# Later seven-product cases in the first phases, none in the last phase, and an earlier scaling of the first tokens

## The chip, the cores and the metric

One NeuronCore of one Trainium2 chip runs the kernel. The metric is the device time of one execution in microseconds (us), as a median of several runs. A hardware profile of one execution stands beside it.

## The reference, cut to what matters

A trunk of two decoder layers over 256 tokens of width 2048, in float32. Only the last step of the second layer, its gated feed-forward, and the final norm are touched:

```
def conv_ffn(h, w_up, cw, cb, w_down):
    a = h @ w_up                                   # 2048 -> 2 x 5632
    c = causal depthwise conv of width 3 over a, + cb
    gate, val = c[..., :D_FF], c[..., D_FF:]
    return (jax.nn.silu(gate) * val) @ w_down      # 5632 -> 2048

x = x + conv_ffn(rmsnorm(x, g_ffn[l]), ...)
return rmsnorm(x, g_final)
```

## The kernel before

Every float32 product is made of three matmuls on split operands: a number is kept as a high part and the rest, and the product is high x high + high x rest + rest x high. A weight chunk of 128 rows and 1024 columns is loaded by SyncE's queue into a `raw` tile (four of them), ScalarE (ACT in the profile) writes its high part `whi` (four tiles), and VectorE (DVE) subtracts to get `wlo` (five tiles).

The feed-forward of the second layer (`ffn(1)`) runs in three parts over the 5632 inner columns (`FF_GROUPS = (4, 4, 3)`, times 512 columns). A part is an up-projection, whose groups end in evictions, convolution, SiLU and a product with the `gate` tile (two of them), and then a down-projection `down_phase`, called twice: phase one makes output columns 0 to 1023, phase two the rest. The down-projection has tokens on the output's partitions. Its inner dimension is taken in cases of 256 rows (eight cases in parts one and two, six in part three), and a case multiplies a 2x2 block matrix of activations (two blocks of 128 tokens, two blocks of 128 rows) with a 2x2 block matrix of weights (two blocks of rows, two halves of 512 columns).

- A plain case makes the eight block products, 24 matmuls of 128x512, into four PSUM banks `e00`, `e01`, `e10`, `e11` (token block, column half). On the weights it costs two ACT and two DVE operations of 128x1024 (`parts`, L707 and L708).
- A fast case (`fast_pair`) makes seven products, 21 matmuls, into seven banks (`e00`, `e01`, `e10` and `m1`, `m5`, `m6`, `m7`). Before its weights are split, DVE makes four sums of 128x512 (`xs`, L721); then three chunks of 1024 and one of 512 columns (`we`) are split. Its two weight chunks go to `raw` tiles in the first fast case of phase one, and otherwise to the two `gate` tiles, which are free only after the last product with the gate (`hv`, L872) of the up-projection.
- After a phase's last fast case `between` copies the four m banks to `staged` by ACT (L1358); `combine` adds them to the tokens `xt` by six DVE operations (L1366). Parts one and two postpone `combine` into the next up-projection. In part three phase one runs it with the first eviction, and phase two runs it at once in `between`.
- `evict` (L1385) adds an e bank to `xt`. In part three it also has ACT square the 512 columns (L1401, column block j of four), multiplies them by the final gain (L1405), and at block j = 2 makes most of the variance (L1407, L1408). `finish` scales one token block by its root (two blocks by ACT in L1424, two by DVE in L1425 and L1426) and stores it.

The order of the cases, and which are fast, stands in the table `FF_FAST`: for eight cases and for six, for each phase, the fast cases and the order. Within a down-projection the DMA, ACT and DVE steps on weights are chained in that order (`behind`); everything else, and TensorE's matmuls, is placed by the scheduler that builds the program. Only the last two cases of part three's phase two (`late=2`) are written out by hand: first all their products for `e00`, then `e01`, `e10`, and `e11` in two pieces of 256 columns, each followed by its eviction.

Of the kernel before, what the change touches and what calls it, by code (L numbers as in the profile page):

```python
# [13 lines left out]
ALU = mybir.AluOpType  # L14
# [17 lines left out]
EPS = 1e-6  # L32
FF_GROUPS = (4, 4, 3)
FF_FAST = {
    4: (((2, 3, 4), (0, 1, 2, 5, 3, 6, 7, 4)), ((2, 3, 4), (0, 1, 2, 5, 3, 6, 7, 4))),
    3: (((1, 2), (0, 1, 3, 2, 4, 5)), ((1,), (0, 1, 2, 3, 4, 5))),
}


# [34 lines left out]
class Kernel:  # L74
# [664 lines left out]


    def down_phase(self, dn, col, order, fast, lhs, rhs, pool, fp, between, evict, finish, late=0, late_gains=None):
        mm = self.nc.tensor.matmul
        names = ("m1", "m5", "m6", "m7"), ("e00", "e01", "e10", "e11")
        acc = {n: self.psum() for group in names[::-1] for n in group}
        left, right = slice(0, 512), slice(512, 1024)
        todo = {n: 0 for n in acc}
        for k in order:
            for n in ("m1", "m5", "m6", "m7", "e00", "e01", "e10") if k in fast else names[1]:
                todo[n] += 1 if k in fast else 2
        total = dict(todo)  # L750

        def three(n, x, w, out=None, ends=None):
            (xh, xl), (wh, wl) = x, w
            start, stop = (todo[n] == total[n], todo[n] == 1) if ends is None else ends
            todo[n] -= 1
            o = acc[n] if out is None else out
            mm(o, xh, wh, start=start, stop=False)  # L757
            mm(o, xh, wl, start=False, stop=False)  # L758
            mm(o, xl, wh, start=False, stop=stop)  # L759

        def plain(k, ws, tb, half, **kw):
            cols = (left, right)[half]
            for i, (wh, wl) in enumerate(ws):
                three(f"e{tb}{half}", lhs(2 * k + i, tb), (wh[:, cols], wl[:, cols]), **kw)

        kept = []
        last_fast = [k for k in order if k in fast][-1]
        for n, k in enumerate(order):
            raws = []
            for i in range(2):  # L770
                if k in fast and (col or k != fast[0]):
                    raw = self.tmp(fp, [P, 1024], "gate", 2)
                else:
                    raw = self.wp.tile([P, 1024], F32, tag="raw", name=self.uid("raw"), bufs=4)
                self.behind(self.nc.sync.dma_start(out=raw, in_=dn[(2 * k + i) * P : (2 * k + i + 1) * P, col : col + 1024]))
                raws.append(raw)
            if late_gains is not None and 2 <= n:
                late_gains(n - 2)
            if k in fast:
                names7 = "e00", "e01", "e10", "m6", "m5", "m7", "m1"  # L780
                for name, q, w in zip(names7, (1, 6, 2, 5, 4, 3, 0), self.fast_pair(raws, pool)):
                    three(name, rhs(k, q), w)
                if k == last_fast:
                    between([acc[m] for m in names[0]])
            else:
                ws = self.plain_pair(raws)
                if n < len(order) - late:
                    for tb in range(2):
                        for half in range(2):
                            plain(k, ws, tb, half)  # L790
                else:
                    kept.append((k, ws))
        if not late:
            for tb in range(2):
                for half in range(2):
                    evict(tb, half, acc[f"e{tb}{half}"])
            return
        ET = mybir.EngineType
        with self.tc.manual_schedule(engines={ET.PE, ET.DVE, ET.Activation}):
            for half in range(2):  # L800
                for k, ws in kept:
                    plain(k, ws, 0, half)
                evict(0, half, acc[f"e0{half}"])
            for k, ws in kept:
                plain(k, ws, 1, 0)
            evict(1, 0, acc["e10"])
            finish(0)
            for k, ws in kept[:-1]:
                plain(k, ws, 1, 1)
            k, ws = kept[-1]  # L810
            e, rest = acc["e11"], self.psum()
            for i, (wh, wl) in enumerate(ws):
                three("e11", lhs(2 * k + i, 1), (wh[:, 512:768], wl[:, 512:768]), out=e[:, :256], ends=(False, i == 1))
            evict(1, 1, e, 0)
            for i, (wh, wl) in enumerate(ws):
                three("e11", lhs(2 * k + i, 1), (wh[:, 768:], wl[:, 768:]), out=rest[:, 256:], ends=(i == 0, i == 1))
            evict(1, 1, rest, 1)
            finish(1)
# [491 lines left out]
class Tokens:  # L1310
# [45 lines left out]
    def between(self, accs):  # L1356
        for i, acc in enumerate(accs):
            self.nc.scalar.activation(self.staged[:, self.ph, i, :], acc, AF.Copy)  # L1358
        if self.last and self.ph:
            self.combine(1)  # L1360
        else:
            self.waiting.append(self.ph)

    def combine(self, ph):
        xt, m = self.xt, self.staged[:, ph]
# [10 lines left out]
        waiting, self.waiting = self.waiting, []  # L1376
        return {2 + 3 * i: [lambda ph=ph: self.combine(ph)] for i, ph in enumerate(waiting)}

    def evict(self, tb, half, acc, piece=None):
        k, nc, xt, sums = self.k, self.nc, self.xt, self.sums  # L1380
        j = 2 * self.ph + half
        c0, n = (0, 512) if piece is None else (256 * piece, 256)
        c = slice(j * 512 + c0, j * 512 + c0 + n)
        o = xt[:, tb, c]
# [9 lines left out]
        part, r, q, v, gb = self.part, self.r, self.q, self.v, self.gb  # L1394
# [6 lines left out]
            nc.scalar.activation(junk[:, :n], o, AF.Square, accum_out=sums[:, tb, j : j + 1])  # L1401
        if piece == 0:
            add(xt[:, tb, j * 512 + 256 : (j + 1) * 512], acc[:, 256:])
        if j < 3:
            nc.vector.tensor_tensor(o, o, gb[:, c], ALU.mult)  # L1405
        if j == 2:
            nc.vector.tensor_reduce(one(part), sums[:, tb, 0:3], AX.X, ALU.add)  # L1407
            nc.vector.tensor_scalar(one(part), one(part), -0.5 / D, -0.5 * EPS, ALU.mult, ALU.add)  # L1408
            nc.scalar.activation(one(r), one(part), AF.Sqrt, scale=-2.0)
        if j == 3:  # L1410
            if piece != 1:
                total = one(part) if piece == 0 else one(v)
                nc.vector.tensor_scalar(total, sums[:, tb, 3:4], -0.5 / D, one(part), ALU.mult, ALU.add)
            if piece == 0:
                return
            nc.scalar.activation(one(r), one(v), AF.Sqrt, scale=-2.0)
            nc.vector.reciprocal(one(r), one(r))
            nc.vector.scalar_tensor_tensor(one(q), one(r), one(r), one(v), ALU.mult, ALU.mult)
            nc.vector.scalar_tensor_tensor(one(r), one(q), 1.5, one(r), ALU.add, ALU.mult)
# [36 lines left out]
```

## Time and profile before

| | |
|---|---|
| median of 3 runs | 2053.24 us (2052.44 to 2053.37) |
| the profiled execution, its own time | 2053.55 us |
| its span from first to last instruction | 2051.8 us |
| mean granted TensorE clock | 0.997 |
| busy: TensorE matmul, VectorE, ScalarE, GpSimd | 99%, 73%, 54%, 7% |
| first down-projection matmul of part one, of part three | 1496.66 us, 1969.56 us |
| last matmul of the kernel, start | 2042.20 us |

Times are microseconds from the span's start. A row of the timeline gives start, duration, engine (PE is TensorE, SPq SyncE's queue), line and operation, and in brackets how long the engine had been idle and what ended that. Matmuls are pipelined, so a matmul's own duration is longer than the distance from one start to the next. A row of the chain gives start, length and what the chain ran through.

### The profile page before, as it was taken

The numbers are of one execution on the slowest core, as the hardware profiler recorded it, in microseconds if no ns is written. First come the engines' busy times: TensorE is split into PE (matmuls) and PEld (weight loads), VectorE is DVE, ScalarE is ACT, GpSimd is POOL, SyncE is SP. The second block draws the span as 40 slices with busy tenths as digits, with TensorE's granted clock in tenths as the row PEclk, the third lists the DMA queues.
The fourth block names the chain that finished last, engine by engine and source line by source line (L and its number), as shares of the span: only waits on it lengthen the run. The fifth ranks groups of instructions, "written<-read, shape, count | busy, mean of one in ns | idle before, by whom it ended". The sixth has DMA issues, their size and how long they took to land.

```text
span 2051.8 us, 39921 instructions
## 1 busy us (share of the span) xinstructions
PE 2034.3 (99%) x16229; PEld 1965.7 (96%) x16229; DVE 1504.8 (73%) x2280; ACT 1113.9 (54%) x1611; POOL 142.5 (7%) x200
## 2 busy tenths in 40 slices
PE   9999999999999999999999999999999999999997
PEld 8989999999999999999999999999988999889986
DVE  5866767767656766557788787777788777888778
ACT  6754744555435555345555675455555555555555
POOL 0000013000000000000043241300000000000000
PEclk9999999999999999999999999999999999999999
DMA  8876556666666666666665634678756666657653
GB/s 246 237 214 184 165 193 190 195 195 195 195 194 189 197 194 195 195 195 192 195 191 183 181 119 156 187 204 215 215 195 192 200 195 195 204 184 204 193 189 134
DMA packets 234253, 394.68 MB, mean 192 GB/s; under 512 B 53902, under 2 KB 61396, under 8 KB 234068
## 3 DMA queue, kind: packets, MB, share of 16 engines
q1 hardware_dynamic: 233876, 391.58, 63.6%
q8 instruction: 127, 2.08, 0.4%
q14 instruction: 58, 0.48, 0.1%
q10 hardware_dynamic: 192, 0.54, 0.1%
HBM read 387.88 MB, written 2.10 MB: 190 GB/s over the span
## 4 chain that ended last, share of the span: by engine, by line
PE 94%; DVE 3%; ACT 1%; DMA 1%; issue 0%; ACTq 0%
PE ps L156 26%; PE ps L157 26%; PE ps L159 26%; PE ps L758 2%; PE ps L759 2%; PE ps L757 2%; PE ps L188 2%; PE ps L189 2%; PE ps L190 2%; DVE wlo L708 1%; PE ps L523 1%; DVE xs L721 1%; DMA gate<-in_w_ffn_down 1%; ACT whi L707 0%; PE ps L603 0%
## 5 line engine op out<-in xcount | busy, mean ns | idle before, releaser
L118 DVE TENSOR_TENSOR wlo<-raw,whi 128x1024 fp32r<-128x1024 f32 x572 | 710.4, 1245 | 385.3 <-ACT whi L117 380.8
L117 ACT ACTIVATE whi<-raw 128x1024 fp32r<-128x1024 f32 x572 | 607.0, 1062 | 687.2 <-PE ps L157 586.6
L156 PE MATMUL ps<-xhl,whi 128*128 128x256 f32 x3264 | 762.8, 277 | 0.0
L157 PE MATMUL ps<-xhl,whi 128*128 128x256 f32 x3264 | 761.4, 276 | 0.0
L156 PEld LDWEIGHTS ps<-xhl,whi 128*128 128x128 f32 x3264 | 612.9, 188 | 0.4
L157 PEld LDWEIGHTS ps<-xhl,whi 128*128 128x128 f32 x3264 | 612.7, 188 | 0.4
L159 PE MATMUL ps<-xhl,wlo 128*128 128x256 f32 x3264 | 436.5, 276 | 0.0
L159 PEld LDWEIGHTS ps<-xhl,wlo 128*128 128x128 f32 x3264 | 400.5, 188 | 0.0
L156 PE MATMUL ps<-h,whi 128*128 128x256 f32 x704 | 163.6, 276 | 0.0
L157 PE MATMUL ps<-h,whi 128*128 128x256 f32 x704 | 163.6, 276 | 0.0
L157 PEld LDWEIGHTS ps<-h,whi 128*128 128x128 f32 x704 | 131.9, 188 | 0.0
L156 PEld LDWEIGHTS ps<-h,whi 128*128 128x128 f32 x704 | 131.9, 188 | 0.0
L156 PE MATMUL ps<-mainhl,whi 128*128 128x256 f32 x512 | 119.6, 277 | 0.0
L157 PE MATMUL ps<-mainhl,whi 128*128 128x256 f32 x512 | 119.4, 277 | 0.0
L853 ACT ACTIVATE c<-a,cT 128x256 f32<-128x256 f32 x176 | 99.2, 589 | 6.6 <-DVE a L236 6.5
L157 PEld LDWEIGHTS ps<-mainhl,whi 128*128 128x128 f32 x512 | 96.0, 188 | 0.0
L156 PEld LDWEIGHTS ps<-mainhl,whi 128*128 128x128 f32 x512 | 95.9, 188 | 0.0
L159 PE MATMUL ps<-h,wlo 128*128 128x256 f32 x704 | 94.1, 276 | 0.0
L758 PE MATMUL ps<-wlo,h 128*128 128x512 f32 (+1 forms) x228 | 89.5, 393 | 1.3 <-DVE wlo L708 1.3
L708 DVE TENSOR_TENSOR wlo<-raw,whi 128x1024 fp32r<-128x1024 f32 x61 | 73.5, 1222 | 21.8 <-ACT whi L707 21.3
L759 PE MATMUL ps<-whi,h 128*128 128x512 f32 (+1 forms) x228 | 89.1, 391 | 0.0
L707 ACT ACTIVATE whi<-raw 128x1024 fp32r<-128x1024 f32 x61 | 64.1, 1057 | 43.8 <-PE ps L759 20.8
(372 smaller groups left out, 2732.0 us busy)
## 6 DMA issues: line engine op xcount, KB each, us to landing
raw<-in_w_ffn_up SPq DMA_DIRECT2D x352, 512.0 KB, 4.2
raw<-in_w_ffn_down SPq DMA_DIRECT2D x152, 512.0 KB, 4.6
raw<-in_w_out SPq DMA_DIRECT2D x64, 512.0 KB, 4.5
raw<-in_w_in_a SPq DMA_DIRECT2D x56, 512.0 KB, 4.5
raw<-in_w_mem_kv SPq DMA_DIRECT2D x31, 512.0 KB, 4.8
gate<-in_w_ffn_down SPq DMA_DIRECT2D x24, 512.0 KB, 7.0
raw<-in_w_in_b SPq DMA_DIRECT2D x16, 512.0 KB, 4.6
raw<-in_w_kv_a SPq DMA_DIRECT2D x9, 512.0 KB, 5.0
```

The source lines that it names most:

```text
L117: nc.scalar.activation(hi[:, :n], raw[:, :n], AF.Copy)
L118: nc.vector.tensor_tensor(lo[:, :n], raw[:, :n], hi[:, :n].bitcast(F32), ALU.subtract)
L156: mm(acc[:, :S], wh, x[:, :S], start=first, stop=False)
L157: mm(acc[:, :S], wh, x[:, S:], start=False, stop=False)
L159: mm(acc[:, :S], wl, x[:, :S], start=False, stop=last)
L188: mm(acc, xh, wh, start=first, stop=False)
L189: mm(acc, xh, wl, start=False, stop=False)
L707: self.behind(self.nc.scalar.activation(hi, w, AF.Copy))
L708: self.behind(self.nc.vector.tensor_tensor(lo, w, hi.bitcast(F32), ALU.subtract))
L758: mm(o, xh, wl, start=False, stop=False)
L759: mm(o, xl, wh, start=False, stop=stop)
L853: nc.scalar.activation(c, a, AF.Identity, scale=w(2), bias=w(3))
```

## The change

Three things change. The order in phase one: with eight cases the fast ones move from places 2, 4 and 7 (counted from 0) to places 3, 5 and 7; with six cases from places 1 and 3 to places 2 and 5. Part three's phase two, which had case 1 fast, has no fast case, so that it allocates only the four e banks, `between` isn't called there, and `combine` isn't run for it. And in the tail `finish(0)` moves into the eviction of `e10`, behind ACT's square and ahead of the gain and the variance; the gain of that block moves behind the variance.

```diff
 FF_FAST = {
-    4: (((2, 3, 4), (0, 1, 2, 5, 3, 6, 7, 4)), ((2, 3, 4), (0, 1, 2, 5, 3, 6, 7, 4))),
-    3: (((1, 2), (0, 1, 3, 2, 4, 5)), ((1,), (0, 1, 2, 3, 4, 5))),
+    4: (((2, 3, 4), (0, 1, 5, 2, 6, 3, 7, 4)), ((2, 3, 4), (0, 1, 2, 5, 3, 6, 7, 4))),
+    3: (((1, 2), (0, 3, 1, 4, 5, 2)), ((), (0, 1, 2, 3, 4, 5))),
 }
...
-        acc = {n: self.psum() for group in names[::-1] for n in group}
+        acc = {n: self.psum() for group in (names[::-1] if fast else names[1:]) for n in group}
...
-        last_fast = [k for k in order if k in fast][-1]
+        last_fast = [k for k in order if k in fast][-1:]
...
-                if k == last_fast:
+                if k in last_fast:
                     between([acc[m] for m in names[0]])
...
-            evict(1, 0, acc["e10"])
-            finish(0)
+            evict(1, 0, acc["e10"], meanwhile=lambda: finish(0))
...
     def between(self, accs):
         for i, acc in enumerate(accs):
             self.nc.scalar.activation(self.staged[:, self.ph, i, :], acc, AF.Copy)
-        if self.last and self.ph:
-            self.combine(1)
-        else:
-            self.waiting.append(self.ph)
+        self.waiting.append(self.ph)
...
-    def evict(self, tb, half, acc, piece=None):
+    def evict(self, tb, half, acc, piece=None, meanwhile=lambda: None):
...
-        if j < 3:
+        meanwhile()
+        if j < 3 and not (tb and j == 2):
             nc.vector.tensor_tensor(o, o, gb[:, c], ALU.mult)
         if j == 2:
             nc.vector.tensor_reduce(one(part), sums[:, tb, 0:3], AX.X, ALU.add)
             nc.vector.tensor_scalar(one(part), one(part), -0.5 / D, -0.5 * EPS, ALU.mult, ALU.add)
             nc.scalar.activation(one(r), one(part), AF.Sqrt, scale=-2.0)
+            if tb:
+                nc.vector.tensor_tensor(o, o, gb[:, c], ALU.mult)
```

On VectorE, in phase one of part one, the last read of the up-projection's gate tile (`hv_2548`) stood behind the whole splitting of fast case 2, whose last row is the first one here, and behind a split of case 5.

```order
L708 TENSOR_TENSOR wlo_2580_18854<-xs_2572_18836,whi_2579_18853 128x1024
L855 SCALAR_TENSOR_TENSOR c_2547_18743<-a_2546_18741,cT_75,c_2547_18743 128x254
L872 TENSOR_TENSOR hv_2545_18737<-gate_2472_18194,c_2544_18733 128x256
L708 TENSOR_TENSOR wlo_2584_18883<-raw_2581_18878,whi_2583_18882 128x1024
L872 TENSOR_TENSOR hv_2548_18747<-gate_2472_18194,c_2547_18743 128x256
L708 TENSOR_TENSOR wlo_2586_18887<-raw_2582_18880,whi_2585_18886 128x1024
```

Now the same place reads as follows; the two L708 rows are the splits of plain case 5.

```order
L708 TENSOR_TENSOR wlo_2573_18837<-raw_2570_18832,whi_2572_18836 128x1024
L854 SCALAR_TENSOR_TENSOR c_2547_18743<-a_2546_18741,cT_75,c_2547_18743 128x254
L708 TENSOR_TENSOR wlo_2575_18841<-raw_2571_18834,whi_2574_18840 128x1024
L721 TENSOR_TENSOR xs_2578_18872<-raw_2576_18868 128x512
L721 TENSOR_TENSOR xs_2578_18872<-raw_2576_18868,raw_2577_18870 128x512
L245 TENSOR_TENSOR hx_2235_16487<-hv_2545_18737,hx_2235_16487 128x256
L871 TENSOR_TENSOR hv_2548_18747<-gate_2472_18194,c_2547_18743 128x256
L721 TENSOR_TENSOR xs_2579_18873<-xs_2578_18872,raw_2577_18870 128x512
L245 TENSOR_TENSOR hx_2235_16487<-hv_2548_18747,hx_2235_16487 128x256
L721 TENSOR_TENSOR xs_2579_18873<-xs_2579_18873,raw_2577_18870 128x512
```

The last gate read has moved ahead of fast case 2's four splits, and behind the splits of case 5 and two of case 2's four sums.

On SyncE's queue, in phase one of part three, the loads of the final gain (`gb`) stand between those of the weights; the two `gate` loads are the second fast case's.

```order
L775 DMA gate_24146<-in_w_ffn_down 128x1024
L775 DMA gate_24148<-in_w_ffn_down 128x1024
L1354 DMA gb<-in_g_final 128x512
L775 DMA raw_24197<-in_w_ffn_down 128x1024
L775 DMA raw_24199<-in_w_ffn_down 128x1024
L1354 DMA gb<-in_g_final 128x512
L775 DMA raw_24234<-in_w_ffn_down 128x1024
L775 DMA raw_24236<-in_w_ffn_down 128x1024
```

Now the two plain cases' loads stand first.

```order
L775 DMA raw_24146<-in_w_ffn_down 128x1024
L775 DMA raw_24148<-in_w_ffn_down 128x1024
L1353 DMA gb<-in_g_final 128x512
L775 DMA raw_24183<-in_w_ffn_down 128x1024
L775 DMA raw_24185<-in_w_ffn_down 128x1024
L1353 DMA gb<-in_g_final 128x512
L775 DMA gate_24220<-in_w_ffn_down 128x1024
L775 DMA gate_24222<-in_w_ffn_down 128x1024
```

The gate loads have moved behind four raw loads, those of plain cases 4 and 5.

On VectorE in the tail, from the eviction of `e10` to those of `e11` (`ps` names are the banks):

```order
L1385 TENSOR_TENSOR xt<-ps_24295,xt 128x512
L1405 TENSOR_TENSOR xt<-xt,gb 128x512
L1407 TENSOR_REDUCE fpart<-fsums 128x1
L1408 TENSOR_SCALAR fpart<-fpart 128x1
L1425 TENSOR_SCALAR xt<-xt,froot 128x512
L1426 SCALAR_TENSOR_TENSOR xt<-xt,froot,gb 128x512
L1385 TENSOR_TENSOR xt<-ps_24296,xt 128x256 x2
```

After the change (lines shifted by the edit):

```order
L1381 TENSOR_TENSOR xt<-ps_24295,xt 128x512
L1424 TENSOR_SCALAR xt<-xt,froot 128x512
L1425 SCALAR_TENSOR_TENSOR xt<-xt,froot,gb 128x512
L1404 TENSOR_REDUCE fpart<-fsums 128x1
L1405 TENSOR_SCALAR fpart<-fpart 128x1
L1408 TENSOR_TENSOR xt<-xt,gb 128x512
L1381 TENSOR_TENSOR xt<-ps_24296,xt 128x256 x2
```

The two scalings of `finish(0)` have moved directly behind the eviction, ahead of the variance and the gain.

## The prediction

> **What bounds the kernel now.** I read the page first, then TensorE's waits, then its timeline at each wait, and last the chain at those places. The page says that TensorE is nearly always at work and that the chain that ended last runs through it.
>
> ```profile
> PE 2034.3 (99%) x16229; PEld 1965.7 (96%) x16229; DVE 1504.8 (73%) x2280; ACT 1113.9 (54%) x1611; POOL 142.5 (7%) x200
> PE 94%; DVE 3%; ACT 1%; DMA 1%; issue 0%; ACTq 0%
> ```
>
> So a change can gain only where TensorE idles or is slow, or behind its last matmul. These are all the waits of TensorE from 1400 us to the end, by who ended them:
>
> ```profile
> PE ps L757 <- ACT whi L707: 5.0, 4, 2.5
> PE ps L758 <- DVE wlo L708: 1.3, 1, 1.3
> PE ps L757 <- ACT staged L1358: 0.2, 1, 0.2
> ```
>
> The timeline has them at six places, all in the second layer's down-projections (the brackets), between the first and the last matmul of part three, and two rows of an undisturbed stretch:
>
> ```profile
> 1519.36 0.74 PE L757 MATMUL ps<-whi,h 128*128 128x512 f32 x2 [0.75 <-ACT whi L707]
> ...
> 1777.54 0.74 PE L757 MATMUL ps<-whi,h 128*128 128x512 f32 x2 [0.70 <-ACT whi L707]
> ...
> 1969.56 0.40 PE L757 MATMUL ps<-whi,h 128*128 128x512 f32 x1
> ...
> 1987.85 0.73 PE L757 MATMUL ps<-whi,h 128*128 128x512 f32 x2 [2.47 <-ACT whi L707]
> ...
> 1989.93 0.79 PE L757 MATMUL ps<-whi,h 128*128 128x512 f32 x1 [1.05 <-ACT whi L707]
> ...
> 2017.52 0.51 PE L757 MATMUL ps<-whi,h 128*128 128x512 f32 x1 [0.23 <-ACT staged L1358]
> ...
> 2033.46 0.51 PE L758 MATMUL ps<-wlo,h 128*128 128x512 f32 x1 [1.28 <-DVE wlo L708]
> ...
> 2036.13 0.39 PE L757 MATMUL ps<-whi,h 128*128 128x512 f32 x1
> ...
> 2040.66 0.39 PE L759 MATMUL ps<-whi,h 128*128 128x512 f32 x1
> 2040.89 0.28 PE L757 MATMUL ps<-whi,h 128*128 128x256 f32 x1
> ...
> 2042.20 0.28 PE L759 MATMUL ps<-whi,h 128*128 128x256 f32 x1
> ```
>
> The rows at 2036.13 and 2040.66 are 20 undisturbed matmuls apart: 4.53 / 20 = 0.2265 us for each. Part three has 138 + 141 matmuls, six of them split into twelve of 256 columns. 273 x 0.2265 + 1.31 us for the twelve (11 steps to the last start, 2040.89 to 2042.20) is 63.15 us, but from 1969.56 to 2042.20 it took 72.64. **Part three loses 9.5 us**, of which the brackets name 5.0. Much of the rest is the clock, the last column but two here (it is 1.00 in the stretches around):
>
> ```profile
> 1989.00:1996.00 7.00, 6.07 (x15) 4.78 (x16) 6.08 (x6) 4.31 (x5) 0.00 (x0) 0.51 0.87 329
> ```
>
> What lies behind the waits is in the chain, and in SyncE's row for the two gate loads:
>
> ```profile
> 1511.69 4.40 DMA gate<-in_w_ffn_down
> 1516.12 1.31 DVE xs L721 x2
> ...
> 1519.36 0.74 PE ps L757 x2
> ```
> ```profile
> 1966.61 16.46 SPq L775 DMA_DIRECT2D gate<-in_w_ffn_down x2
> ```
> ```profile
> 1982.30 0.42 DVE L872 TENSOR_TENSOR hv<-gate,c 128x256 f32<-128x256 f32 x1
> ...
> 1986.68 0.69 DVE L721 TENSOR_TENSOR xs<-gate,gate 128x512 f32<-128x512 f32 x1 [3.06 <-DMA gate<-in_w_ffn_down]
> ```
>
> The second fast case can't load before VectorE's last product with the gate tile; that product stands behind the first fast case's splits; the load takes 3.9 to 4.4 us; then sums and splits follow. This is what ends last at the first four places.
>
> **The change part by part.** Durations of VectorE's rows, from all of the second layer's down-projections (starts follow some 0.08 us sooner than durations say):
>
> ```profile
> L708 DVE TENSOR_TENSOR wlo<-raw,whi 128x1024 fp32r<-128x1024 f32 x61 | 73.5, 1222 | 21.8 <-ACT whi L707 21.3
> ...
> L854 DVE SCALAR_TENSOR_TENSOR c<-a,cT,c 128x255 f32<-128x255 f32 x60 | 27.3, 478 | 0.0
> ...
> L1366 DVE TENSOR_TENSOR xt<-xt,staged 128x1024 f32<-128x1024 f32 x12 | 14.6, 1216 | 0.0
> ...
> L721 DVE TENSOR_TENSOR xs<-gate 128x512 f32<-128x512 f32 x12 | 8.2, 684 | 0.0
> ```
>
> *Parts one and two, first phases.* The last work of the up-projection, the last gate read of part one, and all engines' share of the time around them:
>
> ```profile
> 1496.18 0.76 DVE L236 TENSOR_TENSOR a<-ps,rbc 128x256 f32<-128x256 f32 x2 [0.63 <-PE ps L159]
> ...
> 1511.24 0.42 DVE L872 TENSOR_TENSOR hv<-gate,c 128x256 f32<-128x256 f32 x1
> ```
> ```profile
> 1494.00:1526.00 32.00, 31.25 (x150) 25.99 (x150) 28.59 (x44) 17.88 (x24) 0.00 (x0) 1.00 0.57 196
> ```
>
> Ahead of the last gate read VectorE now has, from 1496.18, three splits (1.14 each, 3.4 us), eight convolution steps (0.40, 3.2), eleven short operations (0.34, 3.7) and two sums (1.2): 11.5 us, to about 1508 instead of 1511.7. The load lands near 1512.5. TensorE starts case 3 after four plain cases and one fast, 117 matmuls or 26.5 us from the part's first at 1496.66: 1523.2, not 1517.7. The splits of case 3 are then held only by free `whi` tiles, and are over by 1523.5, while the last of them is needed at 1527. Both waits go, each with its slow restart (0.74 us for two matmuls instead of 0.45): **1.0 us each, 2.0 in all**. What is late next is case 4, whose gate tiles now come free only one plain case ahead: free at about 1521, landed 1525.5, summed 1530, split by 1534, needed from 1533.4 (first operand) to 1537. If nothing goes, 0; that is the other bound.
>
> *Part three, phase one.* VectorE's 15.3 us of work from 1969.2 to the last gate read put it at 1984.5, two later than before; the load lands at 1988.5. But the second fast case now starts after 117 matmuls, 1996.1, instead of 69. Its third operand gets a `whi` tile only when case 4 and most of 5 are through, at 1995.4; plus 1.06 (ACT) and 1.22 (DVE) it is ready at 1997.7, and needed 17 matmuls into the case, 1999.9. So both waits and the half clock go.
>
> *Part three, the seam.* The m banks are now done only at the phase's end. By the order the new `e00` takes the old `e00`'s bank, and `e01`, `e10`, `e11` those of m1, m6 and m5, which ACT's copies free:
>
> ```profile
> L1358 ACT ACTIVATE staged<-ps x24: 575/598/607, 1537.5 to 2023.5; 128x512 f32<-128x512 f32 x24
> ```
>
> m1 is copied by 1999.8, m6 by 2000.3, m5 by 2001.8; TensorE wants their banks at 2001.8, 2002.7 and 2005.6. I take 0. The bounds are 0 and all four copies, 2.4 us. `combine` (4.7 us of VectorE) runs beside the first plain cases, whose splits it delays by less than their lead.
>
> *Part three, phase two.* 24 matmuls stand for 21: 3 x 0.2265 = **0.7 us more**. VectorE loses four sums, a split and a half, and `combine`, which delayed the split at 2033.46; the copies at 2017.52 go too. What comes next is the pair of last cases for `e00`: by the order the `whi` tiles for case 5 come free four matmuls and one matmul before they start. Two ACT splits and a DVE split later the last `wlo` is there 2.8 us into the stretch, and is wanted after ten matmuls, 2.3: **0.5 us stays**. The bounds are 0 and the 1.5 of today (1.28 and the restart). So of 9.5 us, 9.0 go.
>
> *The tail.*
>
> ```profile
> 2039.73 0.69 DVE L1385 TENSOR_TENSOR xt<-ps,xt 128x512 f32<-128x512 f32 x1
> ...
> 2041.21 0.69 DVE L1405 TENSOR_TENSOR xt<-xt,gb 128x512 f32<-128x512 f32 x1 [0.79 <-ACT fjunk L1401]
> ...
> 2042.08 0.48 DVE L1425 TENSOR_SCALAR xt<-xt,froot 128x512 f32<-128x512 f32 x1
> 2042.47 0.75 DVE L1426 SCALAR_TENSOR_TENSOR xt<-xt,froot,gb 128x512 f32<-128x512 f32 x1
> 2043.13 0.75 DVE L1385 TENSOR_TENSOR xt<-ps,xt 128x256 f32<-128x256 f32 x2
> ```
>
> VectorE waited 0.79 us for ACT's square, then did gain, variance and both scalings before `e11`'s first piece, which TensorE had finished at 2041.8. The two scalings, 1.05 us, now fill that wait; the variance starts 0.2 late (2041.4), and `e11` starts at about 2042.4. ACT does its two scalings right behind the square too, so its square of `e11` comes as much sooner: **0.75 us** less. The bounds are 0, if the last piece's matmul ends the chain, and 1.0.
>
> *Sum.* 2.0 + 9.0 - 0.7 + 0.75 = 11.05. The profiled execution took 2053.55 (span 2051.8 and 1.75 around it), 0.31 above the median: 2042.5 in its terms, **2042.2 as a median**.
>
> **A rule beside the rows.** The clock fell after idles of 2.47 and 1.05 us, with 0.51 granted for 7 us, so what a wait of that size costs is by the rows itself plus about 3.4 us. The Trainium skill, "TensorE: Matmul & The Clock Gate", section on HAM oscillation, says that gaps in TensorE's work longer than about 3.4 us are what bring the half clock back. This trace differs: no single gap here was that long. By the page a wait of 2.5 us left in part three would cost only itself.
>
> **The rivals.** *The second fast case stays late in part three.* VectorE may fall behind its work as counted (it was busy 28.6 of 32 us around 1510), or a load may take longer. A wait of 2.5 us and its half clock, 5.9 us, then stay: 2048.1. Against it speaks that VectorE's long idle at that place was for the load, 3.06 us, and that the lead is now 2.2 us and more. 10%. By the page's rule it would be 2044.7, inside the forecast's range.
>
> *The gate tiles' round trip becomes the bound.* In parts one and two only case 7 (24 matmuls, 5.4 us) lies between fast cases 3 and 4. From the split that frees the gate tile the way is load 4.4, sums 2.4, ACT 1.06, DVE 1.22: 9.1 us. If that split comes only when TensorE starts case 7, and not 6 us ahead as I count, TensorE waits 3.6 us, and with the half clock 7.0, in each part: 2042.2 + 14.1 = 2056.3, slower. From a split about 2.5 us ahead of case 7 downward there is a wait. 4%.
>
> *The change does not do what it says.* The waits move by a place and come back nearly whole at the next fast case and at the seam (2.4 us of copies, and half clock): about 2050.5. 4%.
>
> **How the numbers follow.** The forecast holds 82%. With all waits gone and the tail at its best it is 2041.4; with three quarters of each upper bound taken up (2.0, 2.4, 1.0 and 0.75 us, in all 6.15) it is 2046.8. The runs before lie within 0.9 us of each other, so half of that is put outside the best case: the range is 2040.8 to 2047.0 and leaves out the rivals' 18%. A measurement of this kernel tells 0.2% (4.1 us) from no change: faster means below 2049.1. Faster 0.90 (the forecast and most of the first rival), same 0.05, slower 0.05.
>
> **What would show it.** In the profile after: no bracket on TensorE in the first phases of the three parts, and 1.00 as the clock from 1985 to 2000; the first and last matmul of part three some 64 us apart; one wait of half a microsecond for `wlo` near the start of the last `e00` stretch; `e11`'s first eviction less than 0.3 us behind the end of its matmuls plus VectorE's list. Wrong would make it a wait for `staged` or for a gate load, above all with a clock below 1.00 behind it.

## The result and the profile after

The changed kernel takes **2041.88 us** (median of 4 runs, 2041.44 to 2042.59), the kernel before 2053.12 us in the same comparison: a ratio of 0.9946 with a 95% interval of 0.9929 to 0.9963. A second comparison gave 2041.60 against 2052.15 us, 0.9951 (0.9939 to 0.9964). The forecast was 2042.2 us.

The page of the changed kernel, its engines and the chain that ended last:

```profile
PE 2028.9 (99%) x16232; PEld 1962.7 (96%) x16232; DVE 1496.1 (73%) x2268; ACT 1110.4 (54%) x1605; POOL 142.5 (7%) x200
...
PE 98%; DVE 0%; ACT 0%; DMA 0%; issue 0%; SPq 0%; ACTq 0%
```

TensorE has three matmuls more, VectorE twelve and ACT six instructions fewer. The share of busy time, 99%, says nothing of the gain; the waits do. This is the whole table of TensorE's waits from 1400 us on, where there were three rows with 6.5 us:

```profile
PE ps L758 <- DVE wlo L708: 0.2, 1, 0.2
```

The timeline of TensorE in the changed kernel: the first down-projection matmul of part one, that of part three, the two late splits at the last `e00`, and the last matmul:

```profile
1495.53 0.40 PE L757 MATMUL ps<-whi,h 128*128 128x512 f32 x1
...
1966.30 0.40 PE L757 MATMUL ps<-whi,h 128*128 128x512 f32 x1
...
2020.73 0.39 PE L757 MATMUL ps<-whi,h 128*128 128x512 f32 x1
2021.26 0.50 PE L758 MATMUL ps<-wlo,h 128*128 128x512 f32 x1
...
2021.83 0.40 PE L757 MATMUL ps<-whi,h 128*128 128x512 f32 x1
2022.39 0.50 PE L758 MATMUL ps<-wlo,h 128*128 128x512 f32 x1 [0.17 <-DVE wlo L708]
...
2031.09 0.28 PE L759 MATMUL ps<-whi,h 128*128 128x256 f32 x1
```

From these rows, with the ends of the two spans (2039.9 and 2051.8 us), three stretches are measured that don't depend on when the kernel got going. The stretch from part three's first matmul to the last matmul is called part three below, and what follows the last matmul's start the tail:

| stretch | before | after | gain |
|---|---|---|---|
| start of part one's first down-projection matmul to that of part three's | 472.90 | 470.77 | 2.13 |
| that one to the start of the last matmul | 72.64 | 64.79 | 7.85 |
| start of the last matmul to the end of the span | 9.60 | 8.81 | 0.79 |

Together 10.8 us. The spans differ by 11.9: the other 1.1 us lie ahead of part one's first down-projection matmul (1496.66 and 1495.53), where both kernels have the same instructions. In the ten profiles below whose kernels differ only behind it, that matmul starts anywhere from 1495.20 to 1496.47 us. So its start strays by this much without any difference ahead of it, and the 1.1 us are not counted as a gain. The differences of the medians in the two comparisons, 11.2 and 10.6 us, lie on either side of 10.8.

The clock is whole now where it was half (1989 to 1996 us had 0.51), and TensorE has no idle time in the two stretches in which it waited:

```profile
1494.00:1526.00 32.00, 32.00 (x150) 26.76 (x150) 28.46 (x44) 17.82 (x23) 0.00 (x0) 1.00 0.56 184
1985.00:2000.00 15.00, 15.00 (x68) 12.43 (x67) 12.39 (x16) 9.56 (x12) 0.00 (x0) 1.00 0.59 203
```

### The profile page after: what moved, and what is told of

It is laid out like the page before. It is cut to its first block, busy times and chain, and to the rows that moved or that the text cites. A ratio compares the mean times of both kernels' runs of the same rounds, so it can differ in the third digit from the quotient of the medians.

```text
span 2039.9 us, 39921 instructions
## 1 busy us (share of the span) xinstructions
PE 2028.9 (99%) x16232; PEld 1962.7 (96%) x16232; DVE 1496.1 (73%) x2268; ACT 1110.4 (54%) x1605; POOL 142.5 (7%) x200
## 4 chain that ended last, share of the span: by engine, by line
PE 98%; DVE 0%; ACT 0%; DMA 0%; issue 0%; SPq 0%; ACTq 0%
PE ps L156 26%; PE ps L157 26%; PE ps L159 26%; PE ps L758 4%; PE ps L759 4%; PE ps L757 4%; PE ps L188 2%; PE ps L189 2%; PE ps L190 2%; PE ps L523 1%; PE ps L603 0%; PE ps L601 0%; PE ps L602 0%; PE ps L1206 0%; DMA raw<-in_w_mem_kv 0%; PE ps L995 0%
## 5 line engine op out<-in xcount | busy, mean ns | idle before, releaser
L708 DVE TENSOR_TENSOR wlo<-raw,whi 128x1024 fp32r<-128x1024 f32 x63 | 76.5, 1222 | 26.8 <-ACT whi L707 25.9
```

The costliest lines, as they stand in the source:

```text
L708: self.behind(self.nc.vector.tensor_tensor(lo, w, hi.bitcast(F32), ALU.subtract))
```

## The experiments

Each comparison by time is with the kernel before, on the same chip. Since most differences are below what the times resolve, each run's profile is read as in the table above: the stretch of parts one and two, part three, the tail.

| run | parts 1, 2 | part 3 | tail |
|---|---|---|---|
| before | 472.90 | 72.64 | 9.60 |
| changed | 470.77 | 64.79 | 8.81 |
| changed, again | 470.77 | 64.80 | 8.78 |
| eight-case order alone | 470.77 | 73.17 | 9.59 |
| six-case order alone | 472.73 | 69.60 | 9.65 |
| no fast case in the last phase, alone | 472.65 | 70.57 | 9.64 |
| tail alone | 472.68 | 72.33 | 8.75 |
| fast cases adjacent | 472.45 | 64.80 | 8.78 |
| second fast case one earlier | 470.77 | 65.84 | 8.73 |
| last case in its own tiles | 470.77 | 63.90 | 8.73 |
| the same, again | 470.78 | 63.90 | 8.76 |
| the same, case 2 of the last phase fast | 470.77 | 67.88 | 8.79 |

### The four parts of the change, one by one

**The eight-case order alone.**

```diff
-    4: (((2, 3, 4), (0, 1, 2, 5, 3, 6, 7, 4)), ((2, 3, 4), (0, 1, 2, 5, 3, 6, 7, 4))),
+    4: (((2, 3, 4), (0, 1, 5, 2, 6, 3, 7, 4)), ((2, 3, 4), (0, 1, 2, 5, 3, 6, 7, 4))),
```

> The eight-case order alone on the kernel before. Theory of separate waits: the two idles of TensorE in parts one and two go with their slow restarts; from the first down-projection matmul of part one to that of part three it takes 470.8 us in place of 472.9; part three (72.6 us from its first to its last matmul) and the tail (9.6 us from the start of the last matmul to the end of the span) stay as they were: about 2051.0. Rival, the gate tiles' round trip: the wait only moves to case 4, which has one case ahead of it: no gain, or 3.6 to 7 us more in each part, 2053 to 2067.

Measured: 2050.09 against 2052.29 us, ratio 0.9990 (0.9981 to 0.9999). Both waits of parts one and two are gone and 2.13 us with them, as in the full change. So this term is the order's alone. Part three, whose code is untouched, came out 0.5 us longer. Its phase one was 1.1 us shorter (36.92 us from its first matmul to its last, against 38.02), because the half clock lasted less long; the section on the clock comes back to it. Its phase two was 1.6 us longer: VectorE waited for a gate load that the kernel before has in time there, and then TensorE for a split behind it. Why that load was later isn't shown.

```profile
2003.62 0.69 DVE L721 TENSOR_TENSOR xs<-gate,gate 128x512 f32<-128x512 f32 x1 [1.10 <-DMA gate<-in_w_ffn_down]
```
```profile
2016.06 0.50 PE L758 MATMUL ps<-wlo,h 128*128 128x512 f32 x1 [1.09 <-DVE wlo L708]
```

**The six-case order alone**, phase two's fast case left in.

```diff
-    3: (((1, 2), (0, 1, 3, 2, 4, 5)), ((1,), (0, 1, 2, 3, 4, 5))),
+    3: (((1, 2), (0, 3, 1, 4, 5, 2)), ((1,), (0, 1, 2, 3, 4, 5))),
```

> The six-case order of phase one alone on the kernel before, with case 1 of phase two still fast. Theory of separate waits: of part three's 9.5 us the 7.2 of phase one go (2.6 and 1.3 in the two waits, 3.3 in the half clock behind them); but the four m banks of phase one are now copied at the seam, right ahead of phase two's own fast case, whose sums and splits stand beside combine on VectorE: 1 to 3 us come back there: 2047 to 2049. Rival one, that the fast case of phase two was no burden: nothing comes back, 2045.9. Rival two, that the seam collides fully: a wait of over 2.5 us and the half clock come again there, 2051 to 2053.

Measured: 2049.16 us, ratio 0.9982 (0.9973 to 0.9991); part three 3.0 us shorter. The waits of phase one and their half clock are gone (in the kernel before they take 6.9 us more than its matmuls need at 0.2265 us each), so some 4 us came back, between the theory's 3 and the second rival. By the same count TensorE loses 2.2 us at the seam, where it lost 0.8, and 4.1 at the last `e00`, where it lost 1.6. The chain of this kernel shows what happens at the seam. For some twelve microseconds it runs through VectorE, through `combine` (L1366), the fast case's sums (L721) and splits (L708) in turn:

```profile
1998.95 1.22 DVE wlo L708
2000.17 1.20 DVE xs L721 x2
2001.37 0.60 DVE staged L1366
...
2003.17 0.60 DVE xt L1366
...
2009.51 1.22 DVE wlo L708
2010.73 0.61 DVE xt L1385
```

And the second `combine` makes the split at the last `e00` later than it was (1.73 us, 1.28 before). Two rows of TensorE's timeline, and the clock behind them (columns: length, TensorE's busy time first, the clock last but two):

```profile
2027.01 0.50 PE L758 MATMUL ps<-wlo,h 128*128 128x512 f32 x1 [1.73 <-DVE wlo L708]
...
2028.15 0.52 PE L758 MATMUL ps<-wlo,h 128*128 128x512 f32 x1 [0.17 <-DVE wlo L708]
```
```profile
2025.10:2028.50 3.40, 1.49 (x6) 0.80 (x6) 3.40 (x4) 0.00 (x0) 0.00 (x0) 1.00 0.00 0
2028.50:2031.90 3.40, 3.40 (x10) 2.63 (x9) 2.24 (x5) 1.96 (x3) 0.00 (x0) 0.50 0.02 5
```

**No fast case in the last phase, alone**, with the old orders and the old tail.

```diff
-    3: (((1, 2), (0, 1, 3, 2, 4, 5)), ((1,), (0, 1, 2, 3, 4, 5))),
+    3: (((1, 2), (0, 1, 3, 2, 4, 5)), ((), (0, 1, 2, 3, 4, 5))),
...
-        acc = {n: self.psum() for group in names[::-1] for n in group}
+        acc = {n: self.psum() for group in (names[::-1] if fast else names[1:]) for n in group}
...
```

> Only the fast case of part three's phase two is removed, with the old orders and the old tail. Theory of separate waits: the two losses behind it (0.7 us for the copies to staged, 1.5 for the late wlo) go, three matmuls (0.7) are added and about 0.8 stays at the last e00: 0.7 us less, 2052.4; the waits and the half clock near 1988 us stay. Rival: the copies and the late split were not due to the fast case: 0.7 us slower, 2053.8.

Measured: 2051.00 us, ratio 0.9996 (0.9988 to 1.0005), which times alone don't tell from nothing. In the trace part three is 2.1 us shorter, not 0.7. The wait for `staged` and the 1.28 us for `wlo` are gone, and 0.63 us stays at the last `e00` (0.31 and 0.32). But the half clock near 1990 us lasted 3.4 us in place of 6.8: phase one, whose code the edit doesn't touch, took 36.85 us from its first matmul to its last in place of 38.02. These 1.2 us have nothing to do with the edit, which is worth the other 0.9, close to the 0.7 expected.

**The tail alone.**

```diff
-            evict(1, 0, acc["e10"])
-            finish(0)
+            evict(1, 0, acc["e10"], meanwhile=lambda: finish(0))
...
```

> Only the earlier scaling of the first tokens. Theory of separate waits: from the start of the last matmul to the end of the span 8.8 us in place of 9.6, all else as before: 2052.3. Rival: the last piece's matmul and its eviction set the end, so the move changes nothing: 9.6, 2053.1.

Measured: 2051.31 us, ratio 0.9999 (0.9990 to 1.0007); the tail takes 8.75 us in place of 9.60, and parts one to three are within 0.3 us of before. The rival is out.

The four gains read from the traces are 2.1, 3.0, 2.1 and 0.85; without the 1.2 us of the clock in the third they are 6.9 in sum, and together the parts bring 10.8. The difference lies in part three, 3.9 apart and 7.85 together: the six-case order alone has its gain eaten by the fast case of phase two, and the removal of that case alone leaves the waits of phase one. **The two are one change.**

### How much room the new places have

**The fast cases adjacent**, which makes the prediction's slower rival as bad as the table of orders can.

```diff
-    4: (((2, 3, 4), (0, 1, 5, 2, 6, 3, 7, 4)), ((2, 3, 4), (0, 1, 2, 5, 3, 6, 7, 4))),
+    4: (((2, 3, 4), (0, 1, 5, 2, 6, 7, 3, 4)), ((2, 3, 4), (0, 1, 2, 5, 3, 6, 7, 4))),
```

> The changed kernel with the eight-case order of phase one ending in 6, 7, 3, 4, so that no plain case lies between the last two fast cases. By the changed kernel's trace VectorE's last read of case 3's gate tiles comes 1.7 us ahead of case 3's first matmul, and a gate load takes 5.9 us to land, sums and splits 3.7 to the first wlo: in each part TensorE waits about 3 us at case 4's first wlo and 0.5 to 1 us at a later split. Theory one (the slower rival of the prediction, with the half clock behind such a wait): 7 us in each part, 14 us over the changed kernel, 2056. Theory two (the wait alone costs its own length): 3.5 to 4 us in each part, 2049.5. Theory three (the gate tiles come free early enough): no wait, 2042.

Measured: 2043.58 us, ratio 0.9959 (0.9945 to 0.9973). Parts one and two take 1.7 us more than in the changed kernel, 0.84 each; theories one and two are both far too dear, and theory three (no wait) comes nearest. VectorE's rows show why: the last read of case 3's gate tile is over at 1524.5, 3.2 us ahead of that case's first matmul at 1527.66 and not 1.7, and the second product with the reloaded tile waits only 0.27 us:

```profile
1523.79 0.68 DVE L708 TENSOR_TENSOR we<-gate,we 128x512 fp32r<-128x512 f32 x1
...
1530.55 0.69 DVE L721 TENSOR_TENSOR xs<-gate,gate 128x512 f32<-128x512 f32 x1 [0.27 <-DMA gate<-in_w_ffn_down]
```

From free tile to the landing of both loads it took 6.1 us. And on TensorE four matmuls that need only high parts (L757) stand ahead of the first that needs a new `wlo`, so that a split may come later than the case's start:

```profile
1531.06 1.42 PE L757 MATMUL ps<-whi,h 128*128 128x512 f32 x4
1532.31 0.39 PE L758 MATMUL ps<-wlo,h 128*128 128x512 f32 x1
```

**The second fast case one place earlier.**

```diff
-    3: (((1, 2), (0, 3, 1, 4, 5, 2)), ((), (0, 1, 2, 3, 4, 5))),
+    3: (((1, 2), (0, 3, 1, 4, 2, 5)), ((), (0, 1, 2, 3, 4, 5))),
```

> The changed kernel with the second fast case of the six-case order one place earlier (0, 3, 1, 4, 2, 5). By the changed kernel's trace the gate load lands near 1986.5 us and the first wlo of the case is there at 1989.6, while TensorE would reach the case at 1987.5: a wait of about 2 us and perhaps 0.5 at a later split. Theory: 2 to 2.5 us slower than the changed kernel, 2044.2, or 2047.5 if the half clock follows. Rival: a load or a product with the gate comes as much earlier as the case does, no wait, 2041.9.

Measured: 2043.03 us, ratio 0.9956 (0.9942 to 0.9969); part three 1.05 us longer than in the changed kernel, with one wait more:

```profile
PE ps L757 <- ACT whi L707: 0.7, 1, 0.7
```

The direction was right, the size half of what was expected, and no half clock came. So the last place is needed, but for about one microsecond.

**The last case in its own tiles.**

```diff
...
-            out.append((self.split_tile("whi", True), self.split_tile("wlo", True)))
+            hi = self.split_tile("whi", True) if own is None else self.tmp(own, [P, 1024], "xs", 2, F32R)
+            out.append((hi, self.split_tile("wlo", True)))
...
-                ws = self.plain_pair(raws)
+                ws = self.plain_pair(raws, pool if late and n == len(order) - 1 else None)
```

> The changed kernel with the high parts of the last plain case of part three's phase two in the two xs tiles, which no fast case uses there any more, in place of two whi tiles. If the 0.85 us that stay at the last e00 are due to the four whi tiles, both waits for wlo near 2021 and 2022 us go and it is 0.8 us faster than the changed kernel, 2041.1. Rival: the loads or VectorE are late there too, and nothing changes, 2041.9.

Measured: 2040.70 against 2051.64 us, ratio 0.9946 (0.9932 to 0.9959). TensorE has no wait left from 1400 us to the end, and part three takes 63.90 us, 0.9 less than in the changed kernel:

```profile
1965.97 0.40 PE L758 MATMUL ps<-whi,h 128*128 128x512 f32 x1
...
2029.87 0.28 PE L760 MATMUL ps<-xs,h 128*128 128x256 f32 x1
```

ACT's rows in the changed kernel and then in this one show the cause: the last two splits waited 3.70 us for a matmul to free a `whi` tile; now they follow their loads.

```profile
2014.13 1.06 ACT L707 ACTIVATE whi<-raw 128x1024 fp32r<-128x1024 f32 x1 [0.97 <-PE ps L759]
2018.89 2.01 ACT L707 ACTIVATE whi<-raw 128x1024 fp32r<-128x1024 f32 x2 [3.70 <-PE ps L759]
```
```profile
2015.13 1.06 ACT L707 ACTIVATE xs<-raw 128x1024 fp32r<-128x1024 f32 x1 [0.28 <-DMA raw<-in_w_ffn_down]
2016.44 1.06 ACT L707 ACTIVATE xs<-raw 128x1024 fp32r<-128x1024 f32 x1 [0.24 <-DMA raw<-in_w_ffn_down]
```

It and the changed kernel were run once more together. (Where the expectations below say 63.8 us and 1.0 us, the last matmul but one was read for the last; it is 63.90 and 0.9.)

> The changed kernel once more, to compare it with the next kernel under the same conditions: 10.9 to 11.2 us below the kernel before, ratio 0.9946.

> The kernel with the last plain case's high parts in the xs tiles once more, beside the changed kernel: its part three took 63.8 us against 64.8, so 1.0 us below the changed kernel; if that was chance, 0.

Measured: 2041.60 and 2041.49 us against 2052.15, ratios 0.9951 (0.9939 to 0.9964) and 0.9949 (0.9935 to 0.9962). The trace repeats the 0.9 us in part three to the hundredth (64.80 and 63.90); the times can't tell 0.05% apart. It is the better kernel by its trace, not by a measured time.

**Case 2 of the last phase fast**, on top of the own tiles.

```diff
-    3: (((1, 2), (0, 3, 1, 4, 5, 2)), ((), (0, 1, 2, 3, 4, 5))),
+    3: (((1, 2), (0, 3, 1, 4, 5, 2)), ((2,), (0, 1, 2, 3, 4, 5))),
...
     def between(self, accs):
...
+        if self.last and self.ph:
+            self.combine(1)
...
```

> The kernel with the last case's high parts in the xs tiles, with one fast case put back in part three's phase two, case 2 in place of case 1, two plain cases behind the seam. Theory one (the seven-product case hurt only because it came right behind the seam): three matmuls fewer, 0.7 us less, part three 63.1 us. Theory two (its four copies, combine and sums ahead of the last cases bring waits wherever it stands): 1 to 3 us more in part three.

Measured: 2044.07 us, ratio 0.9966 (0.9952 to 0.9979); part three 67.88 us, 4.0 more than without it though it has three matmuls fewer. Theory one falls. The largest wait is again for a split behind `combine`; VectorE was without a break there:

```profile
2018.01 2.35 DVE L708 TENSOR_TENSOR wlo<-raw,whi 128x1024 fp32r<-128x1024 f32 x2
2020.28 0.68 DVE L1366 TENSOR_TENSOR staged<-staged 128x512 f32<-128x512 f32 x1
2020.88 0.68 DVE L1366 TENSOR_TENSOR xt<-xt,staged 128x512 f32<-128x512 f32 x1
2021.48 2.35 DVE L708 TENSOR_TENSOR wlo<-raw,xs 128x1024 fp32r<-128x1024 f32 x2
```

### What the half clock depends on

In the kernel before and in the runs of its parts the same two idles near 1988 us (about 2.5 and 1 us) were followed by 6.8 us of half clock in two profiles (before, tail alone) and by 3.4 us in two (eight-case order, no fast case). So their length doesn't decide. Two more kernels make TensorE stop in the first layer's feed-forward, where it has no waits, by writing half of one `wlo` again several times.

```diff
+            for _ in range(again):
+                nc.vector.tensor_tensor(lo[:, :512], raw[:, :512], hi[:, :512].bitcast(F32), ALU.subtract)
             nc.vector.tensor_tensor(lo[:, :n], raw[:, :n], hi[:, :n].bitcast(F32), ALU.subtract)
...
```

> The changed kernel with eleven stops of TensorE of growing length in the first layer's up-projections, where it has none: at one chunk in every sixteen VectorE writes half of wlo again 13, 14, ... 23 times ahead of the real split, so that TensorE waits for that wlo once, alone, some 0.6 us longer each time (about 0 to 6 us). The results are the same. Theory one (from the trace of before): an idle of 2.5 us brings the half clock, one of 1.5 us does not. Theory two (the threshold of 3.4 us for a single idle): idles of 2.5 to 3.3 us leave the clock at 1.00, longer ones bring about 6.6 us of half clock. Theory three: it is the share of work in a stretch of some 3.5 us that counts, so that two idles of 2.5 and 1.0 close together do what a single one of 2.5 does not.

Measured: the steps were mis-sized; the stops came out at 8 to 16 us each, the kernel took 2215.28 us, and the question of 2 to 4 us stayed open. But each stop shows both changes of the clock. In the idle of 10.15 us that ended at 547.35 the clock is 1.00 for the first 3.3 us and then half, and behind it half for 3.4 us of work:

```profile
538.00:540.50 2.50, 0.00 (x0) 0.00 (x0) 2.43 (x5) 0.06 (x1) 0.00 (x0) 1.00 0.57 193
547.40:550.60 3.20, 3.20 (x15) 3.20 (x16) 1.23 (x1) 1.06 (x1) 0.00 (x0) 0.50 0.54 163
551.00:554.00 3.00, 3.00 (x29) 3.00 (x28) 0.87 (x1) 1.06 (x1) 0.00 (x0) 1.00 0.54 162
```

Read at a tenth of a microsecond, the clock changed at 540.5, 550.7, 653.15 and 663.4 us: 3, 30 and 3 times 3.413 us apart. So in these traces it changes only on a fixed grid.

> As the ladder of idles before, with 22 short stops of TensorE in the first layer's up-projections: the half split is written again 2, 3, 4, 5 times in turn, idles of about 0.9 to 3.6 us at places that lie anyhow in the grid on which the clock changed in the first ladder (all its changes lie 3.413 us apart or a multiple of that). Theory one (a threshold of idle length): all idles above one length bring the half clock and none below it. Theory two (the share of work in each stretch of the grid): an idle brings it if it takes more than about half of one 3.41 us stretch, so that an idle of 1.8 us brings it where it lies within one, one of 2.5 us brings none where the boundary halves it, and the half clock lasts 3.4 us or a multiple and costs 1.7 us for each.

Measured: 2048.34 us. Only four stops exceeded a quarter of a microsecond, each an idle of 1.26 us at another place; none brought a half clock. The sizes that would separate the theories weren't reached here either. The runs above do separate them. Cut along the grid that the clock's own changes give, the stretches of the kernel before read (columns: length, TensorE busy first, the clock last but two):

```profile
1985.61:1989.02 3.41, 1.02 (x3) 0.48 (x3) 2.30 (x4) 1.78 (x3) 0.00 (x0) 1.00 0.83 281
1989.02:1992.43 3.41, 2.50 (x6) 2.02 (x7) 3.41 (x4) 2.75 (x3) 0.00 (x0) 0.50 1.02 393
1992.43:1995.84 3.41, 3.41 (x9) 2.64 (x9) 2.65 (x3) 1.54 (x2) 0.00 (x0) 0.50 0.72 264
```

and those with the eight-case order alone:

```profile
1981.20:1984.60 3.40, 1.87 (x9) 1.22 (x7) 0.27 (x2) 0.10 (x1) 0.00 (x0) 1.00 0.81 237
1984.60:1988.00 3.40, 1.33 (x4) 0.78 (x5) 3.37 (x5) 2.90 (x4) 0.00 (x0) 1.00 1.01 314
1988.00:1991.40 3.40, 3.40 (x9) 2.62 (x8) 3.40 (x4) 2.55 (x4) 0.00 (x0) 0.51 0.98 393
```

With case 2 of the last phase fast, the stretch ahead of the half clock and the one at it:

```profile
2021.24:2024.65 3.41, 1.85 (x7) 1.15 (x7) 3.41 (x5) 0.51 (x1) 0.00 (x0) 0.99 0.00 0
2024.65:2028.06 3.41, 3.41 (x9) 2.65 (x9) 3.38 (x6) 1.78 (x3) 0.00 (x0) 0.51 0.02 5
```

A stretch with 1.02, 1.33, 1.49 (six-case order) or 1.85 us of work is followed by one at half clock; one with 1.87 us is not, though some 1.5 us of idle lie in it. Nor is the stretch at the end of the second profile of the changed kernel, with 1.65 us:

```profile
2029.55:2032.96 3.41, 1.65 (x13) 1.40 (x12) 3.04 (x9) 2.17 (x7) 0.00 (x0) 1.00 0.68 265
2032.96:2036.37 3.41, 0.00 (x0) 0.00 (x0) 1.81 (x7) 1.54 (x3) 0.00 (x0) 1.00 0.39 149
```

So the share that decides lies near a half, between 1.5 and 1.9 us of 3.41; these busy times, in which the ends of matmuls are modelled, don't give it more closely. A threshold of idle length alone doesn't fit: with the eight-case order an idle had lasted 1.5 us when a stretch ended at 1984.6, and the clock stayed whole; with case 2 fast no idle was longer than 1.38 us, and it fell. And a stretch at half clock is followed by the full clock only where TensorE worked through nearly all of it: the one with 2.50 us wasn't, nor was one with 2.64 (tail alone), and one with 3.10 was (first ladder, from 772.6 us). In the kernel before the second idle fell into the first half-clock stretch, so the half clock lasted two; with the eight-case order it fell ahead of it, so it lasted one. What an idle costs depends on where it lies in the grid, as theory two (theory three of the first ladder) has it.

## Why the prediction was right

*Where the gain lies.* The prediction put all of it into six places named by TensorE's brackets and the clock, and the tail. The three stretches of the first table gave 2.13, 7.85 and 0.79 us where 2.0, 8.3 (9.0 less 0.7) and 0.75 were forecast: 10.8 against 11.05. The medians differ by 11.2 us (10.6 in the second comparison), which agrees with either within the spread of the times.

*Parts one and two.* VectorE's last gate read was to be over near 1508 us; allowing for the start that came 1.1 us earlier, 1506.9. It is over at 1506.8. Case 4, "late next", was to have its gate tiles free at 1519.9 by the same count, and its loads were issued at 1519.95. The eight-case order alone gave the whole term. One reading in it was off without harm: the prediction set 0.74 us for two matmuls behind a wait against 0.45, but 0.74 is a row's duration, and a row of two undisturbed matmuls reads 0.62 (1991.71 us in the changed kernel). So the restart costs 0.1 us. What is left of the 1.0 us, beyond that and the bracket's 0.75, is idle that the bracket leaves out, because a matmul's own duration is longer than its pace.

```profile
1506.36 0.42 DVE L871 TENSOR_TENSOR hv<-gate,c 128x256 f32<-128x256 f32 x1
```
```profile
1519.95 0.93 SPq L775 DMA_DIRECT2D gate<-in_w_ffn_down  x2
```

*Part three, phase one.* Part three started 3.3 us earlier, so the last gate read was due at 1981.3, and was over at 1981.3. The load was to land 4.0 us later and took 5.2:

```profile
1980.88 0.41 DVE L871 TENSOR_TENSOR hv<-gate,c 128x256 f32<-128x256 f32 x1
...
1986.45 0.69 DVE L721 TENSOR_TENSOR xs<-gate,gate 128x512 f32<-128x512 f32 x1 [0.40 <-DMA gate<-in_w_ffn_down]
```

The lead swallowed that. How much lead there was is shown by the second fast case one place earlier: 24 matmuls, 5.4 us, less ahead of it cost 1.05 us. The first rival (the case stays late) had been given 5.9 us and 10%.

*The seam* was taken at 0, and no wait stands there. This rests on phase two having no fast case: with one in it, TensorE loses 2.2 us there (six-case order alone).

*Phase two* is **the term that was mis-sized**. The prediction said that "0.5 us stays" at the last `e00`, by one late `wlo`. There are two, and part three has 64.79 us against the 63.82 that its 282 matmuls need by the same count (276 x 0.2265 + 1.31): 0.97 us stay. The cause it named, `whi` tiles that come free just ahead of the last case, is shown by the own tiles, which brought part three to 63.90. It counted only the second split. That one cost 0.45 us with its slow restart, as worked; the first misses its matmul as well, and cost 0.42.

*The tail* came out as worked: VectorE's scalings now start right behind the eviction of `e10`, and the first eviction of `e11` follows the list without a wait.

```profile
2028.62 0.69 DVE L1381 TENSOR_TENSOR xt<-ps,xt 128x512 f32<-128x512 f32 x1
2029.23 0.48 DVE L1424 TENSOR_SCALAR xt<-xt,froot 128x512 f32<-128x512 f32 x1
2029.62 0.74 DVE L1425 SCALAR_TENSOR_TENSOR xt<-xt,froot,gb 128x512 f32<-128x512 f32 x1
...
2031.14 0.75 DVE L1381 TENSOR_TENSOR xt<-ps,xt 128x256 f32<-128x256 f32 x2
```

*The rivals.* The gate tiles' round trip was priced at 7 us for each part. Even with two seven-product cases side by side it costs 0.84. Its step that failed is the time at which the split frees the tile, which it set at the start of case 7. In the changed kernel the loads into the freed tiles were issued at 1519.95, 6.9 us ahead of that case's first matmul (1526.84), as the prediction's own count of 6 us had it. That the change doesn't do what it says is ruled out by the first two rows of the table of runs.

*The range.* By its own working its lower end is 2041.0 (2041.4 less half of 0.9), not 2040.8; the measured time lies inside either.

*The clock.* The prediction took an idle of 2.5 us to cost itself and about 3.4 us. In the kernel before the half clock cost 2.9 us: of the 6.9 us that phase one loses, the two idles and their restarts take 4.0. And it isn't a price of the idle: behind the same idles it cost 1.6 and 1.7 us in two other runs (eight-case order alone, no fast case). The sum was not hurt, since all of it went; the rivals' times would have been wrong by up to 1.8 us for each wait. The rule that the prediction quoted from the Trainium skill, "TensorE: Matmul & The Clock Gate", section "HAM oscillation — how this bites in real kernels", gaps of over 3.4 us, is not what decides here: an idle of 1.73 us and one of 0.17 in one stretch of the grid were enough in the run of the six-case order. The Trainium skill, "TensorE: Matmul & The Clock Gate", section "What's actually happening", calls the window free-running and 3413 ns long; the changes of the clock in these runs, 3.413 us apart or a multiple of it, agree.

## What to carry to other kernels

Where one engine is busy 99% of the time, list its waits and cut the run into stretches between instructions that both kernels share: a change of half a per cent, which a time only just shows, falls apart into terms of a microsecond that a trace repeats to a few hundredths, as long as the clock doesn't change within them. Moving work later behind a shared buffer pays if what it then meets is moved too: here neither the new order nor the removal of the last phase's fast case had its full gain without the other. And ask of a saving on a full engine (three matmuls, 0.7 us) what it lays on the engine next to it: each of the two ways of keeping it made part three 4 to 5 us longer (69.60 against 64.79, 67.88 against 63.90) by VectorE's sums and `combine` and the half clock behind their waits.

## What the runs showed of the hardware

The granted clock of TensorE changes on a grid of 3.413 us in these traces. A stretch with 1.5 us of work or less was always followed by one at half clock, a stretch with 1.87 us or more never, and between these it went either way. The half clock ended only after a stretch with nearly unbroken work (3.10 us and more, not 2.64). A stretch of full work at half clock costs 1.7 us, half its length. Two idles close together can do what one of them doesn't: with the eight-case order the last 1.0 us of one and 1.06 of the next fell into one stretch and brought the half clock, and single idles of 1.26 to 1.28 us, seven in these traces, never did. The same pair of idles was followed by 1.6 to 2.9 us of such loss, by where it happened to lie. The eleven times of the six-case order alone fall into two groups, 2047.1 to 2047.7 and 2049.0 to 2049.8 us; one half-clock stretch that comes in some executions and not in others would do that, but only one of them has a trace.

The two loads of 512 KB into the gate tiles took 5.2 us from the free tile to landing in part three, against 4.0 at that place in the kernel before, and 6.1 in part one with the fast cases adjacent, against 4.4 in the chain before. And the start strays by 1.5 us between these twelve profiles, more than some parts of the change are worth: the sixth matmul starts within 0.01 us in all of them, the 501st anywhere from 72.5 to 74.0 us, and part one's first down-projection matmul from 1495.20 to 1496.66. Two profiles of the same kernel were 0.2 and 0.3 us apart; what moves the start isn't shown.
